# A hybrid attention and Hyena backbone on one core: order of work in the filters' network, the gates, the rows of maxima and the value weights

## The chip, the cores and the metric

The kernel runs on one core of one Trainium2 chip. The metric is the device time of one execution in microseconds (us): the median of the runs.

The core has five engines with queues of their own: TensorE (PE, with its weight loads, PEld), VectorE (DVE), ScalarE (ACT), GpSimd (POOL) and SyncE (SP), which here issues nearly all DMAs. Each engine takes its instructions in order and waits where something that the next one needs is not there. All data is float32. Nearly all large products are made in three parts: each operand is split into a rounded high part (a copy to the type float32r) and a low part (the rest, by a subtraction), and high x high, high x low and low x high are summed.

## The reference, cut to what matters

Two layers over 1024 latent tokens of width 1024, with 256 context tokens that only attention reads.

```python
for i in range(2):
    shift, scale, gate = split(silu(c) @ ada_w[i] + ada_b[i], 3)          # modulations
    h_lat = rms_norm(x_lat, norm_w[i]) * (1 + scale) + shift              # h_ctx the same way, layer 0
    if i == 0:   # attention: 8 heads of GQA (2 key heads, rotary) and 8 heads of MLA
        q_a, k_a, v_a, c_q, c_kv, k_pe, g = split(h @ w_in)               # norms, rotary
        o = softmax(q k^T * scale) v          # 1024 queries, 1280 keys, 16 heads
        y = (o * silu(g)) @ w_out
    else:        # Hyena, order 2
        p = h_lat @ w_in                      # three streams with a short convolution, one gate
        z = parts[0]
        for o in range(2):
            z = parts[o + 1] * long_conv(z, k_f[:, o], skip[o])           # by Fourier transforms
        y = (z * silu(gate)) @ w_out
    x_lat = x_lat + gate * y
return rms_norm(x_lat, final_norm_w)

# filters of the long convolutions: a small network over positions, with decays
hid = sin(freq * (emb @ w1 + b1)); hid = sin(freq * (hid @ w2 + b2))
h = (hid @ w3 + b3) * exp(-t * abs(deltas)); kern = kern / sum(abs(kern)); k_f = rfft(kern)
```

## The kernel before

The program runs in stages, and the order of the work on PE, ACT, DVE and POOL is the order in which the instructions are written (or, for the two middle stages, in which a planner of generators hands them out). Only SP's order is left to the compiler's scheduler.

**Filters' network and ada weights (0 to about 32 us).** The positions' network runs on two halves of 512 positions, q = 1 first. sin_arg makes the argument of a Sin in seven DVE instructions (L460 to L466), hidden(q) takes the second Sin on ACT (L504), rounds it (L505) and subtracts for the low part Hl (L506), today on POOL for q = 1 and on DVE for q = 0. taps(n) multiplies the hidden values with the last weights (PE, L479 and L100 to L102); it is run for 32 steps, (p, gq) with p the block of 128 channels. Steps 0 and 1 need half 1 alone. decay makes the exponentials on ACT (L530), decayed the kernel tile on DVE (L535), norms the absolute sums (ACT L544, POOL L546), first_stage and second_stage the two stages of the filters' Fourier transform (PE L557 and L572), regroup and spectra move data by SP's DMAs.

In between, the generator modulations loads sixteen pieces of ada_w, 512 KB each, and multiplies them with silu(c) (PE, L217). It is pulled by hand: pull(mods, m) takes m steps, of which each issues the load of piece j + 4 and the four product records of piece j. PM says how many steps are pulled at four places. The pieces lie in five tiles in turn (tags ckh, ckl, kpe and two of xt), so the load of piece 14 overwrites piece 11, and so on. A row copy (L221), a transposition (L225) and small DVE instructions (L235, L236) end the generator. row_stats loads the ten tiles of token rows (SP L373, the tag xt again) and takes their sum of squares (ACT L380) in steps n = 1 to 10 of the loop over 38 steps n that follows.

**Projection and gates (about 245 to 485 us).** After four chunks of the attention's input projection, gates() makes the gate in 16 steps of 24 products: for step n it loads a weight tile wr of 512 KB (SP, L800), rounds it (ACT, L803) and subtracts for the low part wl (L804), on POOL for n < 8, else on DVE. wr, wh and wl have two buffers each. Beside it run elementwise (norms and the rotary steps of the queries, four pairs of tiles: DVE L922, POOL L838, DVE L839 and L840), latents and stacks, each handed out by the planner S after its yields (a cost on PE, a delay).

**Attention (about 485 to 1008 us).** 32 groups gi of one head and one half of the queries (q = gi % 2), five steps s each: scores(0) and scores(1), two or three products each (L1277), the exponential PT (ACT, L1294), products with the values of earlier PT in bursts of 16 records (L1180), sums of PT on POOL and DVE (L1187 to L1193). Ahead of it the maxima of the next group's scores are taken (PE L989 and L993, DVE L990 and L994), joined by max_all (DVE, L1008) at the end of s = 3, and max_rows, at s = 4, turns them on PE (L1023) and writes them as a row under the next group's queries (DVE, L1028). mla_prep makes the queries, keys and values of MLA beside it; its value weights are rounded (ACT L1506) and the low part uvl is taken on POOL (L1508) ahead of 30 products with the latents.

**Output projection, Hyena (1008 us to the end).** Not touched.

## Time and profile before

| | us |
|---|---|
| median of 3 runs | 1821.87 |
| lowest, highest | 1821.21, 1828.35 |
| the profiled execution | 1821.09 |
| its span, first to last instruction | 1819.3 |
| mean granted TensorE clock | 0.987 of full speed |

The profile is of one execution. The rows below give times from the span's start. "busy" is an engine's time inside instructions; "[0.67 <-DVE m L1008]" behind a row says that the engine stood idle for 0.67 us ahead of it and what ended that. In the rows by stretch the numbers behind the stretch are its length, then each engine's busy time (with its instructions), the granted clock, the DMA engines' busy share and the GB/s that they moved.

### The profile page before, as it was taken

How to read it: one execution, taken by the hardware profiler on the slowest of the kernel's cores; microseconds unless marked ns; L12 is line 12 of the kernel's file. 1: busy time of each engine (PE TensorE's matmuls, PEld its weight loads, DVE VectorE, ACT ScalarE, POOL GpSimd, SP SyncE). 2: the span in 40 equal slices, each digit the busy share in tenths (PEclk: the TensorE clock that was granted, in tenths of full speed). 3: DMA queues.
4: the chain of work that ended last, by engine and by line, in shares of the span. 5: the costliest groups of instructions: out<-in, count | busy, mean ns of one | idle time of the engine just before them, and what ended most of it. 6: DMA issues, size and time to landing. Idle time of an engine off the chain costs nothing.

```text
span 1819.3 us, 25906 instructions
## 1 busy us (share of the span) xinstructions
PE 1725.1 (95%) x9616; PEld 1346.1 (74%) x9616; DVE 1029.7 (57%) x1495; ACT 774.3 (43%) x1326; POOL 865.6 (48%) x615
## 2 busy tenths in 40 slices
PE   7999999998999999899999999999999999899898
PEld 2667789986766666666666788888888788788686
DVE  5557757446666665466565323456657555645743
ACT  5878711243545544544444333243343333332431
POOL 2457712534379777577776453234333333244400
PEclk9999999999999999999999999999999999999999
DMA  7766688232120010100010227568787778787633
GB/s 256 246 211 216 210 257 276 64 82 74 43 56 24 11 47 21 39 32 22 22 34 21 81 88 184 161 178 221 215 228 223 223 217 219 209 239 212 196 98 110
DMA packets 245709, 253.28 MB, mean 139 GB/s; under 512 B 30591, under 2 KB 195367, under 8 KB 245167
## 3 DMA queue, kind: packets, MB, share of 16 engines
q1 hardware_dynamic: 243408, 249.53, 46.4%
q10 hardware_dynamic: 2176, 2.10, 0.4%
q8 instruction: 76, 1.25, 0.3%
q14 instruction: 49, 0.40, 0.1%
HBM read 169.65 MB, written 61.94 MB: 127 GB/s over the span
## 4 chain that ended last, share of the span: by engine, by line
PE 57%; DVE 7%; DMA 5%; POOL 3%; issue 2%; ACT 2%; SPq 1%; DVEq 0%; POOLq 0%; ACTq 0%
PE pw L1277 8%; PE pw L102 8%; PE pw L100 8%; PE pw L101 8%; PE pv L1180 7%; DMA K<-Kd 4%; PE pq L989 3%; PE pq L100 2%; PE pq L101 2%; PE pq L102 2%; PE pq L1871 2%; PE pq L1854 2%; DVE mx L990 2%; PE pq L1212 1%; POOL wl L1712 1%
## 5 line engine op out<-in xcount | busy, mean ns | idle before, releaser
L1294 ACT ACTIVATE PT<-pw 128x1024 f32<-128x1024 f32 x160 | 163.7, 1025 | 171.8 <-PE pw L1277 160.4
L990 DVE TENSOR_REDUCE mx<-pq 128x1 f32<-128x512 f32 x256 | 170.9, 683 | 112.9 <-PE pq L989 111.1
L100 PE MATMUL pw<-h1h,wh 128*128 128x512 f32 x512 | 209.4, 409 | 0.0
L102 PE MATMUL pw<-h1h,wl 128*128 128x512 f32 x512 | 202.7, 396 | 4.4 <-POOL wl L1712 4.4
L101 PE MATMUL pw<-h1l,wh 128*128 128x512 f32 x512 | 201.2, 393 | 0.0
L1847 POOL TENSOR_TENSOR K<-K,skp 128x512 f32<-128x512 f32 x64 | 86.3, 1350 | 217.8 <-DMA K<-Kd 196.1
L1189 POOL TENSOR_TENSOR acc<-acc,PT 128x1024 f32<-128x1024 f32 x62 | 147.5, 2379 | 22.3 <-ACT PT L1294 20.7
L102 PEld LDWEIGHTS pw<-h1h,wl 128*128 128x128 f32 x512 | 96.8, 189 | 26.8 <-POOL wl L1712 5.3
L101 PEld LDWEIGHTS pw<-h1l,wh 128*128 128x128 f32 x512 | 97.0, 189 | 17.8
L546 POOL TENSOR_TENSOR kacc<-kacc,kabs 128x512 f32<-128x512 f32 x56 | 72.4, 1294 | 79.1 <-ACT kabs L544 77.2
L100 PEld LDWEIGHTS pw<-h1h,wh 128*128 128x128 f32 x512 | 97.0, 189 | 17.5
L1712 POOL TENSOR_TENSOR wl<-wr,wh 128x1024 fp32r<-128x1024 f32 x32 | 79.5, 2483 | 54.9 <-ACT wh L1711 54.9
L1857 DVE SCALAR_TENSOR_TENSOR cB<-pq,K 64x512 f32<-64x512 f32 x64 | 44.4, 693 | 107.0 <-DMA K<-Kd 38.5
L1827 ACT COPY caT<-pq 128x512 f32<-128x512 f32 x64 | 37.6, 588 | 146.0 <-PE pq L102 104.0
L1187 POOL TENSOR_TENSOR acc<-PT,PT 128x1024 f32<-128x1024 f32 x31 | 73.9, 2385 | 53.7 <-ACT PT L1294 50.4
L572 PE MATMUL pq<-au,FBk 128*128 128x256 f32 x256 | 68.6, 391 | 11.6 <-DVE kc L583 10.1
L1888 DVE TENSOR_TENSOR cil<-spare,cih 128x512 fp32r<-128x512 f32 x64 | 54.4, 888 | 44.3 <-ACT cih L1887 44.3
L1873 ACT COPY cbT<-pq 128x512 f32<-128x512 f32 x64 | 37.5, 587 | 95.4 <-PE pq L1871 49.7
L1180 PE MATMUL pv<-PT,Va 128*64 128x256 f32 x640 | 77.9, 385 | 0.0
L1180 PE MATMUL pv<-PT,Vm 128*64 128x256 f32 x640 | 77.7, 385 | 0.0
L1854 PE MATMUL pq<-cau,FB 128*128 128x128 f32 x512 | 69.7, 280 | 8.1 <-DVE cA L1860 7.0
L1871 PEld LDWEIGHTS pq<-cA,GB 128*128 128x128 f32 x512 | 68.3, 195 | 11.8 <-issue 6.5
(449 smaller groups left out, 4705.8 us busy)
## 6 DMA issues: line engine op xcount, KB each, us to landing
K<-Kd SPq DMA_DIRECT2D x128, 256.0 KB
au<-aT SPq DMA_DIRECT2D x128, 128.0 KB
space<-in_ada_w_dram SPq DMA_DIRECT2D x32, 512.0 KB
wr<-in_hy_w_in_dram SPq DMA_DIRECT2D x32, 512.0 KB
ad<-caT SPq DMA_DIRECT2D x64, 256.0 KB
cau<-ad SPq DMA_DIRECT2D x32, 512.0 KB
bd<-cbT SPq DMA_DIRECT2D x32, 512.0 KB
spare<-bd SPq DMA_DIRECT2D x64, 256.0 KB
```

The lines of the kernel that those rows point to most:

```text
L100: nc.tensor.matmul(ps, lh, rh, start=start, stop=False)
L101: nc.tensor.matmul(ps, lh, rl, start=False, stop=False)
L102: nc.tensor.matmul(ps, ll, rh, start=False, stop=stop)
L990: nc.vector.reduce_max(m[:, i, j:j + 1], ps, axis=AX.X)
L1180: nc.tensor.matmul(ps[64 * e:64 * e + 64, 0:256], vals[:, 2 * s + j], PT[:, j, 256 * e:256 * e + 256], start=s == 0 and j == 0, stop=s == ...
L1189: eng.tensor_tensor(accs[gi], accs[gi], PT, ALU.add)
L1277: nc.tensor.matmul(ps[:, 512 * j:512 * j + 512], l[:, kt * P:(kt + 1) * P], r, start=i == 0, stop=i == len(passes) - 1)
L1294: nc.scalar.activation(PT, ps.rearrange("p (a q) -> p a q", q=512), AF.Exp, scale=SC_A if kind == 0 else SC_M)
L1712: nc.gpsimd.tensor_tensor(wl, f(r), f(wh), ALU.subtract)
L1847: nc.gpsimd.tensor_tensor(K[:, 0], K[:, 0], B["skp"].unsqueeze(1).to_broadcast([P, 4, P]), ALU.add)
L1854: nc.tensor.matmul(ps[:, i * P:(i + 1) * P], FB[:, 4 * uc + i, :], au[:, 4 * (uc % 2) + i, :], start=True, stop=True)
L1871: nc.tensor.matmul(ps[:, i * P:(i + 1) * P], GB[:, 4 * uc + i, :], A1[:, i, :], start=True, stop=True)
```

## The change

It changes the order of work at four places, and the engine of two subtractions. No product and no byte is added or removed.

- The ada steps are pulled later: PM goes from 3, 3, 5, 3 to 2, 1, 3, 3, and the loop's first three turns pull two instead of one. Nine instead of fourteen of the sixteen are ahead of the loop. hidden(1) is moved between the two arguments; the low part of half 1 goes to DVE, that of half 0 to POOL; the split of the first coefficients moves ahead of half 1's argument.
- In gates() the load of step n + 2 is issued at step n, apart from the rounding and subtraction of step n + 1; the low parts 2, 4 and 6 stay on POOL, 1, 3, 5 and 7 go to DVE.
- max_rows stays between scores(0) and scores(1) for even groups and goes behind scores(1) for odd ones. Its planner's cost of 0.1 falls away.
- The low part uvl of the value weights goes from POOL to DVE.

```diff
-PM = 3, 3, 5, 3
+PM = 2, 1, 3, 3
...
-            (nc.vector, nc.gpsimd)[q].tensor_tensor(Hl[:, c], Hr[:, c], f(Hh[:, c]), ALU.subtract)
-
-        args[1] = sin_arg(pss[1], b2)
+            (nc.gpsimd, nc.vector)[q].tensor_tensor(Hl[:, c], Hr[:, c], f(Hh[:, c]), ALU.subtract)
+
         nc.scalar.copy(ind, indr)
         split_coefs(0)
+        args[1] = sin_arg(pss[1], b2)
+        hidden(1)
         args[0] = sin_arg(pss[0], b2)
-        hidden(1)
         hidden(0)
...
-            pull(mods)
+            pull(mods, 2 if n < 3 else 1)
...
-            wt = {}
+            wt, raw = {}, {}
 
             def load(n):
                 if n < 16:
                     i = n % 8
-                    r = wp.tile([P, NK, P], F32, tag="wr", bufs=2, name=nm("wr"))
-                    nc.sync.dma_start(r, win[:, :, 1184 + i * P:1184 + (i + 1) * P])
+                    raw[n] = wp.tile([P, NK, P], F32, tag="wr", bufs=2, name=nm("wr"))
+                    nc.sync.dma_start(raw[n], win[:, :, 1184 + i * P:1184 + (i + 1) * P])
+
+            def split(n):
+                if n < 16:
+                    r = raw.pop(n)
                     wh = wp.tile([P, NK, P], F32R, tag="wh", bufs=2, name=nm("wh"))
                     wl = wp.tile([P, NK, P], F32R, tag="wl", bufs=2, name=nm("wl"))
                     nc.scalar.copy(wh, r)
-                    (nc.gpsimd if n < 8 else nc.vector).tensor_tensor(wl, r, f(wh), ALU.subtract)
+                    (nc.gpsimd if n in (2, 4, 6) else nc.vector).tensor_tensor(wl, r, f(wh), ALU.subtract)
                     wt[n] = wh, wl
 
+            load(1)
             wt[0] = box["g0"][1:]
             for n in range(16):
                 hf, i = divmod(n, 8)
-                load(n + 1)
+                split(n + 1)
+                load(n + 2)
...
-                if s == 4 and gi + 1 < 32:
+                if s == 4 and gi % 2 == 0:
                     max_rows(gi + 1)
-                    cost += 0.1
                 scores(1, todo)
+                if s == 4 and gi % 2 and gi + 1 < 32:
+                    max_rows(gi + 1)
...
-        nc.gpsimd.tensor_tensor(uvl, r, f(uvh), ALU.subtract)
+        nc.vector.tensor_tensor(uvl, r, f(uvh), ALU.subtract)
```

## Rows read from the trace of the kernel before

**Rows 1.** The page: each engine's busy time, share of the span and instructions, and the shares of the lines in the chain of work that ended last.

```profile
PE 1725.1 (95%) x9616; PEld 1346.1 (74%) x9616; DVE 1029.7 (57%) x1495; ACT 774.3 (43%) x1326; POOL 865.6 (48%) x615
...
PE pw L1277 8%; PE pw L102 8%; PE pw L100 8%; PE pw L101 8%; PE pv L1180 7%; DMA K<-Kd 4%; PE pq L989 3%; PE pq L100 2%; PE pq L101 2%; PE pq L102 2%; PE pq L1871 2%; PE pq L1854 2%; DVE mx L990 2%; PE pq L1212 1%; POOL wl L1712 1%
```

**Rows 2.** Busy time by stretch: two of the first 60 us.

```profile
10.00:15.00 5.00, 2.19 (x10) 0.42 (x8) 3.61 (x7) 1.82 (x5) 0.00 (x0) 1.00 1.00 402
...
30.00:60.00 30.00, 27.12 (x144) 17.92 (x145) 14.56 (x19) 28.16 (x71) 15.04 (x13) 1.00 0.74 244
```

**Rows 3.** The timeline of the first 40 us: PE, ACT, DVE, POOL and SP's queue (start, duration, engine, line, operation).

```profile
14.84 0.40 ACT L342 CAST b<-b3r 2x256 fp32r<-2x256 f32 x1
...
16.70 0.81 DVE L460 TENSOR_SCALAR sa<-pq,vecs 128x512 f32<-128x512 f32 x1 [2.92 <-PE pq L497]
...
20.44 1.27 ACT L504 ACTIVATE Hr<-sa 64x512 f32<-64x512 f32 x2 [5.20 <-DVE sa L466]
...
22.93 2.57 POOL L506 TENSOR_TENSOR Hl<-Hr,Hh 128x1024 fp32r<-128x1024 f32 x1 [7.19 <-ACT Hh L505]
...
25.45 0.39 PE L479 MATMUL pw<-b,ind 128*128 128x256 f32 x1
...
26.54 1.27 ACT L504 ACTIVATE Hr<-sa 64x512 f32<-64x512 f32 x2 [3.76 <-DVE sa L466]
...
29.00 0.42 SPq L499 DMA_DIRECT2D FKc<-in_FK_dram  x1
...
31.52 1.23 DVE L535 TENSOR_TENSOR kern<-pw,dec 128x1024 f32<-128x1024 f32 x1 [1.29 <-ACT dec L530]
...
32.51 1.05 PE L217 MATMUL pada<-adaw,sT 128*32 128x512 f32 x4 [1.56 <-DMA adaw<-in_ada_w_dram]
...
33.83 1.27 ACT L530 ACTIVATE dec<-dlt,tng 128x128 f32<-128x128 f32 x4
...
35.48 1.88 PE L557 MATMUL pq<-kern,FKc 128*128 128x512 f32 x4
...
36.53 0.59 ACT L559 COPY aT<-pq 128x512 f32<-128x512 f32 x1 [1.43 <-PE pq L557]
...
39.53 1.06 ACT L380 ACTIVATE xs<-xs 128x1024 f32<-128x1024 f32 x1
```

**Rows 4.** The gates: SP's loads of the weights (their number at the end), the timeline of PE and DVE, and a stretch with the granted clock.

```profile
371.84 87.47 SPq L800 DMA_DIRECT2D wr<-in_w_in_dram  x15
...
413.51 0.80 PE L102 MATMUL pw<-h,wl 128*128 128x512 f32 x1 [3.69 <-POOL wl L804]
...
415.00:420.00 5.00, 5.00 (x15) 3.97 (x14) 2.28 (x3) 0.00 (x0) 4.18 (x5) 0.59 0.32 94
...
419.61 3.40 DVE L840 TENSOR_TENSOR pD<-rt,rt 128x1024 f32<-128x1024 f32 x1 [2.68 <-POOL rt L838]
...
428.13 1.23 DVE L840 TENSOR_TENSOR pD<-rt,rt 128x1024 f32<-128x1024 f32 x1 [2.72 <-POOL rt L838]
...
429.27 1.22 DVE L804 TENSOR_TENSOR wl<-wr,wh 128x1024 fp32r<-128x1024 f32 x1
...
430.55 0.49 PE L102 MATMUL pw<-h,wl 128*128 128x512 f32 x1 [2.70 <-DVE wl L804]
```

**Rows 5.** Attention: PE's waits for the joined maxima, in the first and in the second kind of head (us in total, times, longest); the timeline of PE at two transpositions; the durations of the row's writing (ns, least, median, most; first and last start).

```profile
PE pq L1023 <- DVE m L1008: 4.0, 6, 0.8
...
PE pq L1023 <- DVE m L1008: 2.7, 7, 0.4
...
537.39 0.40 PE L1277 MATMUL pw<-Qa,K 128*128 128x512 f32 x1
...
537.62 0.39 PE L1277 MATMUL pw<-Q,K 128*128 128x512 f32 x1
...
538.69 0.27 PE L1023 MATMUL pq<-ident,m 128*4 128x128 f32 x1 [0.67 <-DVE m L1008]
...
539.36 1.95 PE L1180 MATMUL pv<-PT,Va 128*64 128x256 f32 x16
...
840.45 0.27 PE L1023 MATMUL pq<-ident,m 128*4 128x128 f32 x1 [0.38 <-DVE m L1008]
...
L1028 DVE TENSOR_TENSOR QA<-pq,dneg x16: 682/684/684, 723.6 to 988.7; 4x512 fp32r<-4x512 f32 x16
```

**Rows 6.** The timeline around the value weights' low part, ACT, POOL, DVE and PE, and the stretch behind it with its granted clock.

```profile
740.04 0.60 ACT L1506 CAST uvh<-uvr 128x512 fp32r<-128x512 f32 x1
...
740.28 2.35 POOL L1189 TENSOR_TENSOR acc<-acc,PT 128x1024 f32<-128x1024 f32 x1 [2.54 <-ACT PT L1294]
...
741.23 0.17 DVE L1008 TENSOR_REDUCE m<-mx 128x4 f32<-128x12 f32 x1
...
744.05 1.26 POOL L1508 TENSOR_TENSOR uvl<-uvr,uvh 128x512 fp32r<-128x512 f32 x1
...
745.37 0.79 PE L101 MATMUL pq<-uvl,ckh 128*128 128x512 f32 x1 [4.15 <-POOL uvl L1508]
...
745.00:750.00 5.00, 4.63 (x11) 3.67 (x12) 0.00 (x0) 1.76 (x3) 3.85 (x3) 0.50 0.27 105
```

**Rows 7.** SP's queue: the load that stands in turn 22 of the loop, and the page's line on the loads of the filters' spectra.

```profile
45.81 0.38 SPq L613 DMA_DIRECT2D w<-in_w_in_dram  x1
...
K<-Kd SPq DMA_DIRECT2D x128, 256.0 KB
```

## The prediction

> **What bounds the kernel now.** I read the page first, then the chain of waits, then busy time by stage, then the timeline of the four places that the diff touches. TensorE is busy 95% of the span, and its products hold the largest shares of the chain that ended last [rows 1]. No other engine is near it, so an edit pays only where PE stood still, or ran at half clock, for something that the edit moves. The reader should look for PE's stalls beside each edit. In the first 40 us PE is not the bound: a chain over VectorE, ScalarE and the loads sets the pace, and from 30 to 60 us ScalarE is busy 28.16 of 30 us [rows 2]. In the gates PE waits for a low part twice (3.69 and 2.70 us), the first time followed by half clock [rows 4]. In attention it waits for the maxima of odd groups [rows 5]. Once it waits 4.15 us for the low part of the value weights, and then runs at 1.2 instead of 2.4 GHz [rows 6].
>
> **Head (modulations behind the filters' network).** Today half 1's Sin starts at 20.44, its low part 2.49 us later on GpSimd, taking 2.57, and the first taps at 25.45 [rows 3]. Afterwards VectorE first makes the coefficients' low part (ScalarE's cast ends at 15.24; I take 15.65 for its end), then half 1's argument (16.70 to 20.44, 3.74 us), to 19.4; the low part starts at 21.9 and ends at 23.1 (1.22 on VectorE, as in [rows 4]). The taps come 2.3 us earlier. But half 0's argument now stands behind that low part on VectorE: 23.1 + 3.74 = 26.85 against 26.54 today. So the first kernel tile comes 0.3 us later and ends at 33.1 instead of 32.75. No gain has reached ScalarE yet.
>
> Next, the product that waited 1.56 us for ada weights at 32.51 no longer stands ahead of the first-stage products: they start at 33.1 instead of 35.48. ScalarE's copies of them come after the next decays (33.83 + 1.27 = 35.1 today, 35.4 then) instead of at 36.53: ScalarE is 1.1 us ahead, and its first sum of squares could start at 38.4 instead of 39.53. But that needs the first token rows, and their load stands in SP's queue behind ada loads. With five tiles, load 14 waits for the product of piece 11, which moves from ahead of the decays to behind the first-stage products: 33.1 + 1.88 + some 0.9 of its 1.05 = 35.9. Today load 14 left just ahead of the one at 29.00, at 28.5, and its product ran at 32.51: 4.0 us. So it lands at 39.9. The token rows behind it are another 0.5 MB, 1.3 us at the 402 GB/s of the best stretch [rows 2]: 41.15. ScalarE stands for 2.7 us and is then **1.6 us later** than today. From there it has hardly a gap to 60 us, so the shift stays. I take +1.6 because written order is what SP's row shows in the head: the table FKc, which needs nothing, left at 29.00 behind the blocked loads. Bounds: -1.1 (row loads pulled ahead) and +2.9 (load 15, 0.5 MB, also in front). The five product steps that move into the loop's first turns, 1.05 us or less each on PE, lie under ScalarE's full stretch: nothing; without that cover 2 us. The generator's end on VectorE moves two turns back, where I see no wait for it: nothing.
>
> The Trainium skill (DMA: Bandwidth & Descriptors, Anatomy of one DMA) gives a load 2.0 us plus its bytes at 436 GB/s, on GpSimd's path; an estimate from it is 3.2 us for 512 KB, where the row has 4.0. By it the head would cost 0.8 instead of 1.6 us.
>
> **Gates.** Loading two steps ahead changes nothing that I can price: SP already spreads the fifteen loads over 87 us, each leaving when its buffer is free [rows 4], and the first, the only one that ScalarE waits for, keeps its place: 0. What counts is that low parts 1, 3, 5 and 7 go from GpSimd to VectorE (1.22 each). PE waits for the chain of rotary steps (VectorE product, four GpSimd products, VectorE sum, the next pair), with the low parts between. A VectorE sum next to a GpSimd low part takes 3.40 us, without one 1.23 [rows 4]. After pairs 0 and 2 this saves 2.17 and adds 1.22: 2 x -0.95. Pair 1 keeps low part 6 on GpSimd. Low parts 1 and 3 stand in front of VectorE's sums of squares and push the start by an estimated 0.25 each: +0.5. Low part 8, at 429.27 today, comes at 427.9: **-1.4 us**, and PE's restart at 430.55 with it. The long stall (3.69) is cut into shorter ones, and the half clock at 415 to 420 should go; neither is added, since the wait for low part 8 lies behind them and would take it back. Queued behind the low parts on VectorE is the next rotary product, which is in the sum. Bounds: 0 (the clock falls again) and -1.9 (no push at the start).
>
> **Rows of maxima.** For odd groups the transposition of the maxima now stands behind both score products instead of between them. Today PE goes 1.07 us from a score product to the transposition, of which the product itself is 0.23: 0.84 lost, 0.67 of it a wait. In the second kind of head the wait is 0.38, so 0.54 lost [rows 5]. There are 6 and 7 such waits; the other transpositions have none and stay or lose nothing. Moved, the second half's products fill the wait: two, 0.47 of 0.84, in the first kind; three, 0.70, all of 0.54, in the second. 6 x 0.47 + 7 x 0.54 = **-6.6 us**. It could hold up the next group's second score product, which needs the row that VectorE writes (0.68 us) after the transposition; between lie 1.95 us of value products: nothing, and 0.3 us a group if the burst weren't there. The planner's charge of 0.1 per group falls away; its other streams restart at group ends, so 0, +-1.
>
> **Low part of the value weights on VectorE.** Its rounded part is ready at 740.64, but GpSimd comes to it at 744.05, behind a sum (740.28, 2.35 us) and a scaling. VectorE is free from 741.40. It would read two tiles of SBUF beside GpSimd's sum, and as in the gates wait for that sum's end, 742.63, then take half of 1.22 for half the columns: 743.25. PE restarts at 743.35 instead of 745.37: -2.0. Its wait shrinks from 4.15 to 2.1 us; after 2.70 the clock stayed up (430.55), after 3.69 it fell [rows 4]. So the half clock should go too: eleven products at 0.42 us [rows 6] instead of 0.23, and the wait's restart, -2.35. Together **-4.35**; bounds -2.0 (clock falls) and -5.5 (no block).
>
> The Trainium skill (Advanced Engine Details and Errata, Mode Summary) says that GpSimd and VectorE's two-port modes block each other. A subtraction of two float32 tensors is in none of these modes; by the letter it would start at once, for 1.2 us more. The rows (3.40 against 1.23) speak for the block.
>
> **Sum.** +1.6 - 1.4 - 6.6 - 4.35 = -10.75. Against the profiled execution's 1821.09 us (span 1819.3) that is 1810.3. The median of the runs lies 0.8 above the profiled one: **1811.1**.
>
> **Rivals.**
> B: SP's order is planned anew, and the token rows' loads go ahead of the blocked ada loads. For it: SP doesn't always follow the text (the load that stands in turn 22 left at 45.81, six us after turn 1's sum of squares) [rows 3, 7]. Head -1.1 instead of +1.6: 1808.4.
> C: waits come back. The clock falls after the shorter stalls too (value weights -2.0, gates 0), and half of the maxima's gain returns as a wait for a buffer or a row: +1.6 - 0 - 3.3 - 2.0 = -3.7, 1818.2. For it: the new stalls in the gates stand closer together. Against it: no other engine in attention is near full [rows 1].
> D: slower than before. With new times in the planner SP's order changes in the second half too, where loads of the filters' spectra hold 4% of the chain [rows 1, 7]. If each of the 64 pairs leaves one place later, each costs one issue, 0.4 us: +25.6, 1836.7. It decides from 27 pairs on; slower by over 0.5% takes 50. Against it: nothing of that half is edited.
>
> **How the numbers follow.** A, the forecast, 0.46 (own range 1808 to 1814); B 0.25; C 0.24; D 0.05. B with the far bounds of the value weights and the gates gives 1805; C gives 1818; about 2 in 10 lie outside. 0.5% (9.1 us) is about what a measurement of this kernel can tell from no change, so faster means under 1812.8: three quarters of A, B, a little of C: 0.62. Slower by over 0.5%: 0.04. Within: 0.34.
>
> **What would show it.** Head: taps at 23, first sum of squares at about 41 after a wait for the token rows (B: 38.4, no wait). Gates: VectorE's sums after pairs 0 and 2 at 1.23 us; PE's restart at step 8 some 1.4 us earlier, counted from the gates' start; clock at its full level throughout. Maxima: no wait at transpositions of the second kind, about 0.3 us in the first. Value weights: low part 2 to 3 us after the cast, then full clock. I am wrong if attention doesn't shrink by about 11 us, or if the head moves by more than 3.

## The result and the profile after

| | before | after |
|---|---|---|
| median of five runs each (us) | 1827.38 | 1811.57 |
| lowest, highest | 1821.21, 1830.2 | 1808.1, 1814.33 |
| profiled execution, its span | 1821.09, 1819.3 | 1808.1, 1806.3 |

The ratio after to before is 0.9933, 95% interval 0.9912 to 0.9955: faster by 0.45 to 0.88%. The median of 1811.57 stands 0.5 us from the 1811.1 predicted. The two medians of the table are 15.8 us apart; with later runs the median of before settles at 1821.5 (of 33 runs, 1813.5 to 1831.0), so the gain is some 10 us. Executions of one kernel spread over 6 us and more; so below, stages are compared over several profiled executions. The profiled execution of x7_value_cover (2101 us at a granted clock of 0.75) and one execution of x11_cover_keys_early (8427 us) are far slower than the rest and are left out, as are two such of before (2223 and 2809 us).

The page of after [for before: rows 1], busy time and chain by engine. PE is busy 95% as before; DVE's busy time is 8.6 us longer, POOL's 14.5 shorter.

```profile
PE 1723.1 (95%) x9616; PEld 1346.7 (75%) x9616; DVE 1038.3 (57%) x1500; ACT 774.5 (43%) x1326; POOL 851.1 (47%) x610
...
PE 64%; DMA 10%; DVE 10%; issue 6%; POOL 5%; ACT 3%; SPq 1%; POOLq 0%; DVEq 0%; ACTq 0%
```

**Head** [rows 2, 3]. The timeline of after, DVE's low part of half 1, PE's first taps, and the first products:

```profile
22.23 1.23 DVE L506 TENSOR_TENSOR Hl<-Hr,Hh 128x1024 fp32r<-128x1024 f32 x1 [2.54 <-ACT Hh L505]
...
23.51 0.58 PE L102 MATMUL pw<-w3h,Hl 128*128 128x256 f32 x1 [0.54 <-DVE Hl L506]
...
26.59 3.72 PE L217 MATMUL pada<-adaw,sT 128*32 128x512 f32 x20
...
33.30 1.98 PE L557 MATMUL pq<-kern,FKc 128*128 128x512 f32 x4 [0.91 <-DVE kern L535]
```

ACT's sums of squares and SP's loads in the same execution, and two stretches (columns as in rows 2; the last three are granted clock, DMA share and GB/s):

```profile
39.94 1.06 ACT L380 ACTIVATE xs<-xs 128x1024 f32<-128x1024 f32 x1 [1.74 <-DMA xs<-in_ctx_dram]
...
50.39 1.06 ACT L380 ACTIVATE xs<-xs 128x1024 f32<-128x1024 f32 x1 [1.49 <-DMA xs<-in_x_dram]
```
```profile
31.08 1.40 SPq L373 DMA_DIRECT2D xs<-in_ctx_dram  x2
36.31 0.82 SPq L199 DMA_DIRECT2D adaw<-in_ada_w_dram  x2
```
```profile
25.00:30.00 5.00, 5.00 (x28) 2.19 (x27) 1.91 (x4) 2.89 (x4) 0.47 (x1) 0.65 0.12 20
35.00:40.00 5.00, 5.00 (x29) 2.71 (x28) 1.74 (x2) 3.26 (x10) 3.48 (x4) 1.00 0.90 352
```

Three things are to be seen. The taps come at 23.5 and the first-stage products at 33.3, as worked out. From 25 to 30 us the DMA engines move 20 GB/s: five ada steps stand behind the taps on PE (26.59), and until they run no tile comes free for a load. And SP did not keep the written order: the first token rows left at 31.08, ahead of the last ada loads (36.31), but were 8.9 us on the way to the sum of squares that waited for them.

**Gates** [rows 4]. DVE's rotary sums and low parts, PE's last wait, and the stretch behind the longest wait:

```profile
401.85 1.23 DVE L846 TENSOR_TENSOR pD<-rt,rt 128x1024 f32<-128x1024 f32 x1 [2.72 <-POOL rt L844]
...
410.71 3.36 DVE L846 TENSOR_TENSOR pD<-rt,rt 128x1024 f32<-128x1024 f32 x1 [2.72 <-POOL rt L844]
419.17 1.23 DVE L846 TENSOR_TENSOR pD<-rt,rt 128x1024 f32<-128x1024 f32 x1 [2.71 <-POOL rt L844]
...
427.78 1.22 DVE L808 TENSOR_TENSOR wl<-wr,wh 128x1024 fp32r<-128x1024 f32 x1
```
```profile
429.05 0.50 PE L102 MATMUL pw<-h,wl 128*128 128x512 f32 x1 [1.60 <-DVE wl L808]
```
```profile
415.00:420.00 5.00, 5.00 (x17) 3.94 (x17) 2.26 (x3) 0.00 (x0) 3.79 (x4) 0.73 0.21 64
```

The sums of pairs 0 and 2 take 1.23 us; pair 1, with low part 6 still on POOL, is held as before. The clock fell again (0.73 here), behind PE's wait of 2.07 us for low part 6.

**Maxima** [rows 5]. PE's waits for the joined maxima from 484 to 727 us (from 752 to 992 there is none in the list), and a transposition of the first kind:

```profile
PE pq L1029 <- DVE m L1014: 1.0, 4, 0.3
```
```profile
536.08 0.40 PE L1283 MATMUL pw<-Q,K 128*128 128x512 f32 x1
536.37 0.17 DVE L1014 TENSOR_REDUCE m<-mx 128x4 f32<-128x12 f32 x1
536.68 0.27 PE L1029 MATMUL pq<-ident,m 128*4 128x128 f32 x1 [0.21 <-DVE m L1014]
536.88 1.95 PE L1186 MATMUL pv<-PT,Va 128*64 128x256 f32 x16
```

**Value weights** [rows 6].

```profile
735.93 2.35 POOL L1195 TENSOR_TENSOR acc<-acc,PT 128x1024 f32<-128x1024 f32 x1 [2.55 <-ACT PT L1301]
...
736.96 1.88 DVE L1515 TENSOR_TENSOR uvl<-uvr,uvh 128x512 fp32r<-128x512 f32 x1
...
738.89 0.79 PE L101 MATMUL pq<-uvl,ckh 128*128 128x512 f32 x1 [2.02 <-DVE uvl L1515]
```

The subtraction ends 0.56 us behind POOL's sum, and the wait is 2.02 instead of 4.15 us. The stretch behind it still has some products at 1.2 GHz, though fewer than in before:

```profile
740.00:745.00 5.00, 5.00 (x20) 4.05 (x19) 0.00 (x0) 3.47 (x6) 3.47 (x2) 0.81 0.28 98
```

**Where the span's 13.0 us went** in this pair of profiles, by the starts of the same ACT instructions: gates reached (first rounded latents) 379.97 and 380.10, +0.1; from there to attention's first exponential 106.45 and 104.79, -1.7; from there to group 16's first exponential 245.94 and 243.11, -2.8; to group 18's first, which holds the value weights and one transposition, 46.98 and 43.47, -3.5; to the output stage's first sum of squares 239.96 and 236.76, -3.2; to the end 800.00 and 798.09, -1.9. The prediction's four places hold -11.1 of it.

### The profile page after: what moved, and what is told of

It is laid out like the page before. It is cut to its first block, busy times and chain, and to the rows that moved or that the text cites. A ratio compares the mean times of both kernels' runs of the same rounds, so it can differ in the third digit from the quotient of the medians.

```text
span 1806.3 us, 25904 instructions
## 1 busy us (share of the span) xinstructions
PE 1723.1 (95%) x9616; PEld 1346.7 (75%) x9616; DVE 1038.3 (57%) x1500; ACT 774.5 (43%) x1326; POOL 851.1 (47%) x610
## 4 chain that ended last, share of the span: by engine, by line
PE 64%; DMA 10%; DVE 10%; issue 6%; POOL 5%; ACT 3%; SPq 1%; POOLq 0%; DVEq 0%; ACTq 0%
PE pw L102 9%; PE pw L1283 9%; PE pw L101 9%; PE pw L100 9%; PE pv L1186 7%; DMA K<-Kd 4%; PE pq L995 3%; PE pq L100 3%; PE pq L101 3%; PE pq L102 2%; DMA Kd<-kc 2%; PE pq L1861 2%; PE pq L1878 2%; PE pq L572 1%; DVE mx L996 1%
## 5 line engine op out<-in xcount | busy, mean ns | idle before, releaser
L1195 POOL TENSOR_TENSOR acc<-acc,PT 128x1024 f32<-128x1024 f32 x62 | 147.3, 2376 | 22.4 <-ACT PT L1301 20.8
```

The lines of the kernel that those rows point to most:

```text
L1195: eng.tensor_tensor(accs[gi], accs[gi], PT, ALU.add)
```

## The experiments

All stages below are measured between the same ACT instructions.

| kernel | fifth sum of squares | gates reached | gates | groups 0 to 15 | groups 16, 17 | groups 18 to 31 | second half |
|---|---|---|---|---|---|---|---|
| before | 57.03 | 379.97 | 106.45 | 245.94 | 46.98 | 239.96 | 800.00 |
| x2_maxima_alone | 56.16 | 379.69 | 108.01 | 243.17 | 44.39 | 236.75 | 802.87 |
| x3_low_parts_alone | 57.82 | 380.65 | 104.85 | 245.95 | 46.20 | 239.88 | 800.79 |
| x4_value_low_part_alone | 61.37 | 379.73 | 108.02 | 245.89 | 41.45 | 239.89 | 796.16 |
| x1_head_undone | 60.77 | 379.56 | 104.82 | 243.21 | 40.93 | 236.76 | 800.82 |
| x6_steps_back | 60.69 | 380.39 | 104.89 | 243.12 | 41.85 | 236.78 | 800.68 |
| x9_together | 60.04 | 381.30 | 103.85 | 243.22 | 44.36 | 236.78 | 807.16 |
| after | 59.42 | 380.10 | 104.79 | 243.11 | 43.47 | 236.76 | 798.09 |
| x0_changed_again | 60.63 | 383.61 | 104.84 | 243.19 | 41.22 | 236.77 | 800.74 |
| x8_low6 | 59.30 | 384.35 | 103.91 | 243.12 | 41.56 | 236.75 | 800.00 |
| x7b_cover_again | 60.02 | 385.27 | 104.83 | 243.21 | 44.30 | 236.78 | 800.03 |
| x11_cover_keys_early | 59.86 | 381.77 | 104.80 | 243.20 | 42.59 | 236.78 | 802.95 |
| x10_all_behind | 59.70 | 378.88 | 104.80 | 246.30 | 41.47 | 236.76 | 799.79 |

The first five rows have the old head, the next two the old steps with the new order of the network, the last six the changed head. Kernels with the same code there repeat within 0.1 us in the gates (but for those of before, 106.45 or 108.0) and in attention (but for groups 16 and 17); the head, the way to the gates and the second half do not.

In the head the seven executions with the ada steps as before (x6 and x9 among them) part from the six with the steps pulled later, by starts in the traces (us):

| | steps as before | steps later |
|---|---|---|
| first-stage products start | 34.5 to 39.8 | 33.2 to 33.4 |
| first sum of squares | 38.6 to 43.8 | 39.0 to 40.5 |
| from the second sum to the third | 4.2 to 5.2 | 6.2 to 7.6 |
| from the seventh to the tenth | 20.0 to 20.4 | 20.8 to 21.6 |
| from the tenth to the gates reached | 288.5 to 293.6 | 288.5 to 294.4 |

**x2_maxima_alone**

```diff
-                if s == 4 and gi + 1 < 32:
+                if s == 4 and gi % 2 == 0:
                     max_rows(gi + 1)
-                    cost += 0.1
                 scores(1, todo)
+                if s == 4 and gi % 2 and gi + 1 < 32:
+                    max_rows(gi + 1)
```

> The kernel before with the rows of maxima alone changed (transposition of odd groups behind both score products, the planner's 0.1 gone). Theory (each wait is filled by the products behind it, 0.47 us in the first kind of head, 0.54 in the second): attention shortens in steps at odd groups, 6.4 us in all, no other stage moves; total about 1815 where the kernel before has 1821. The wait for the value weights' low part stays at 4.15 us and its half clock at about 6.8. Rival C of the prediction (half comes back as waits for a buffer or a row): 3.3 us, total about 1818. Rival (the planner places other work anew without the 0.1): the order on PE changes outside the rows of maxima and the steps are not of one size.

Measured: median 1816.35 against 1821.5 (ratio 0.9967, 0.995 to 0.9984). Groups 0 to 15 are 2.77 us shorter than before, groups 18 to 31 3.21, and PE's waits for the joined maxima are the four of 0.3 us or less that after has. Nothing comes back: rival C falls for this part. The planner did not move other work: in attention PE's instructions start in the same order as in before, but for the fifteen transpositions of odd groups. The wait for the value weights was 2.86 here, not 4.15, with nothing changed there. What varies is the load of these weights. ACT waits for it ahead of the scaling, the cast and the exponential that POOL's sum needs. The first row is of before, the second of x2:

```profile
738.50 0.73 ACT L1502 ACTIVATE uvr<-uvr,kw 128x512 f32<-128x512 f32 x1 [3.85 <-DMA uvr<-in_w_ukv_dram]
...
734.90 0.72 ACT L1503 ACTIVATE uvr<-uvr,kw 128x512 f32<-128x512 f32 x1 [1.75 <-DMA uvr<-in_w_ukv_dram]
```

Counted from group 16's first exponential, the cast starts at 7.67 us in before and at 6.34 here. Over all executions it lies between 6.3 and 7.7, after's profile (7.69) being the latest.

**x3_low_parts_alone**

```diff
-                    (nc.gpsimd if n < 8 else nc.vector).tensor_tensor(wl, r, f(wh), ALU.subtract)
+                    (nc.gpsimd if n in (2, 4, 6) else nc.vector).tensor_tensor(wl, r, f(wh), ALU.subtract)
```

> The kernel before with the engines of low parts 1, 3, 5, 7 of the gates alone changed (DVE instead of POOL); loads as before. Theory (the chain of rotary steps waits less, the order of loads is worth nothing): the whole gain of the gates comes from here: low part 8 at 427.8 instead of 429.3, attention starts 1.5 to 1.65 us earlier than before, the half clock at 413 to 420 shrinks from about 6.8 to 3.4 us; total about 1820 where the kernel before has 1821.5. Rival (the loads two steps ahead brought it): less than 0.3 us here.

Measured: median 1818.38 (ratio 0.998, 0.9959 to 1.0001), which alone is not told apart from before. The gates take 104.85 us, as in after (104.79): the engines bring the whole gain, the loads two steps ahead nothing. The gates of before took 106.45 in its own profile and 108.0 in x2 and x4: there the clock fell after the second wait too. The stretch from 430 to 435 us in before, then in x2:

```profile
430.00:435.00 5.00, 4.45 (x21) 3.68 (x22) 4.08 (x5) 1.16 (x2) 2.05 (x3) 1.00 0.42 109
...
430.00:435.00 5.00, 4.75 (x16) 3.90 (x17) 3.60 (x4) 0.46 (x1) 2.35 (x4) 0.67 0.50 115
```

**x4_value_low_part_alone**

```diff
-        nc.gpsimd.tensor_tensor(uvl, r, f(uvh), ALU.subtract)
+        nc.vector.tensor_tensor(uvl, r, f(uvh), ALU.subtract)
```

> The kernel before with the value weights' low part alone changed (DVE instead of POOL). Theory (the wait shrinks by 2.1 us, but two microseconds are still enough for the clock to fall, for a shorter time): PE restarts 2.5 us after its first product with the rounded part instead of 4.6, the products run at 1.2 GHz for about 3 us instead of 5 to 7, the stage gains 3.0 us; total about 1818.5 where the kernel before has 1821.5. Rival (the prediction's step: the half clock goes with the shorter wait): 4.35 us gained. Rival (here the subtraction starts at another time relative to GpSimd's sum and is held up by it, 3 us or more): 1 us or less.

Measured: median 1819.72 (ratio 0.9988, 0.997 to 1.0007), which alone is not told apart from before. The timeline of POOL, DVE and PE, and the two stretches behind:

```profile
740.25 2.38 POOL L1189 TENSOR_TENSOR acc<-acc,PT 128x1024 f32<-128x1024 f32 x1 [1.23 <-ACT PT L1294]
...
742.52 0.17 DVE L1008 TENSOR_REDUCE m<-mx 128x4 f32<-128x12 f32 x1
742.60 0.69 DVE L1508 TENSOR_TENSOR uvl<-uvr,uvh 128x512 fp32r<-128x512 f32 x1
743.34 0.50 PE L101 MATMUL pq<-uvl,ckh 128*128 128x512 f32 x1 [0.84 <-DVE uvl L1508]
```
```profile
740.00:745.00 5.00, 4.09 (x31) 2.82 (x31) 3.01 (x6) 2.67 (x6) 4.67 (x3) 1.00 0.07 28
745.00:750.00 5.00, 5.00 (x24) 4.12 (x23) 0.00 (x0) 4.34 (x8) 2.94 (x2) 1.00 0.19 77
```

PE goes on at 743.34, where the prediction has 743.35, but that is a coincidence. DVE joins the maxima until then (742.52), and by the time it comes to the subtraction POOL's sum is ending (742.63): nothing holds it, and it takes 0.69 us. PE waits 0.84 us, not 2.1. Group 16 began 1.3 us later than in before, and its load came earlier in the group (ACT waited 2.02 us for it instead of 3.85), so that POOL's sum ran at the same time as in before. Counted from group 16's first exponential, PE goes on at 9.70 us here and in x1, and at 11.70 in x2 and x3, whose load came as early; with the late load it is 10.89 (after) against 13.00 (before). So DVE is worth 2.0 to 2.1 us either way. The clock stays up. Groups 16 and 17 gain 5.5 us on before's profile, of which some 1.3 are the load's. The first theory (half clock after two microseconds) is not put to the test, since no wait was that long.

That the subtraction is held by POOL's sum is seen where it starts beside it, as in after and in x0 (POOL, then DVE):

```profile
738.68 2.36 POOL L1195 TENSOR_TENSOR acc<-acc,PT 128x1024 f32<-128x1024 f32 x1 [1.66 <-ACT PT L1301]
740.59 1.00 DVE L1515 TENSOR_TENSOR uvl<-uvr,uvh 128x512 fp32r<-128x512 f32 x1
```

In seven executions (after, x0, x6, x7b, x8, x10, x11) it starts 0.45 to 1.32 us ahead of the sum's end and takes 1.00 to 1.88 us; each time it ends 0.54 to 0.56 us behind the sum.

**x1_head_undone**

```diff
-PM = 2, 1, 3, 3
+PM = 3, 3, 5, 3
...
-            pull(mods, 2 if n < 3 else 1)
+            pull(mods)
```

and the order and engines of hidden and sin_arg as before.

> The changed kernel with the head as it was before (steps pulled 3, 3, 5, 3, one per turn, order and engines of the filters' network as before); gates, rows of maxima and value weights stay changed. Theory (the head loses: the later ada steps leave the DMA engines empty from 25 to 30 us, 20 GB/s in the changed kernel against 216 before, so token rows come late and ScalarE runs 2.4 us late at 60 us): first square sum at 39.5 instead of 39.9, the one in the seventh place at 53.2 instead of 55.6, end of the filters' stage 1.25 us earlier than in the changed kernel. The half clock ahead of the gates, which lasted about 6.8 us before and 3.4 in the changed kernel, goes with the times of the head and comes back: the gates start within 0.2 us of the changed kernel, and the total stays within 1 us of it (about 1811.6). Rival 1 (the short half clock has nothing to do with the head): the 1.25 us are kept, gates start 1.2 us earlier, total about 1810.3. Rival 2 (the head's change pays somewhere behind the head): gates or attention later by 2 us or more, total 1813.5 or more.

Measured: median 1812.79 of 11 runs from 1800.7 to 1819.6 (ratio 0.9943, 0.9919 to 0.9968). The first sum of squares came at 42.31, not at 39.5, with the very head of before: my theory had read a difference of 2.4 us between two executions as the work of an edit. The gates were reached at 379.56; the long half clock ahead of them did not come back. It is no mark of the old head: it stands in the traces of before, x7b and x11 alone, of which two have the changed head.

**x0_changed_again**: the changed kernel, unedited.

> The changed kernel once more, unedited, to see how far one execution stands from the next. Theory (the head's times are set by when loads land, and differ between executions of the same code by up to 5 us, as five executions with the old head showed: first square sums at 38.6 to 43.8; the projection swallows this, all five reach the gates' first rounded latents at 379.6 to 380.7): the first square sum falls anywhere between 38 and 44, the first rounded latents at 380 +-0.6, from there to attention's first exponential 104.8 +-0.1 (three executions of the changed gates), the wait for the value weights' low part 2.0, with or without half clock behind it. Median within 2 us of 1811.6. Rival (the changed head itself costs 2.4 us at 60 us): the square sums come at the same 39.9 and 54.6 again.

Measured: median 1811.51 (ratio 0.9942, 0.9924 to 0.9961). First sum of squares at 39.75, gates reached at 383.61: the second half of the theory on the head falls, since the projection does not swallow what the head is late, and the first half does not hold for this head, whose first sum came at 39.0 to 40.5 in six executions. The rival has the first sum right (39.9); the sum that it puts at 54.6 came at 55.82. Gates (104.84) and attention repeat; the wait for the value weights was 1.16, with full clock.

**x6_steps_back**

```diff
-PM = 2, 1, 3, 3
+PM = 3, 3, 5, 3
...
-            pull(mods, 2 if n < 3 else 1)
+            pull(mods)
```

> The changed kernel with the ada steps alone pulled as before (3, 3, 5, 3, one per turn); the new order and engines of the filters' network stay. Theory (the steps pulled late empty the DMA engines from 25 to 30 us, and the head as a whole is swallowed by the projection): over 150 GB/s from 25 to 30 us where the changed kernel has 20; the first rounded latents at 380 +-0.6 all the same; median within 2 us of the changed kernel's. Rival 1 (late steps are worth what the medians of the first three parts leave over, 1.2 us): median 1.2 us above the changed kernel. Rival 2 (they cost 2.4 us): median 2.4 below it, gates reached at 377.7.

Measured: median 1810.9 (ratio 0.9941, 0.9924 to 0.9957); no difference in the median against x0, on the same chip. The stretch from 25 to 30 us moves 224 GB/s: the hole was made by the late steps.

```profile
25.00:30.00 5.00, 3.87 (x28) 2.09 (x24) 1.89 (x4) 2.91 (x4) 0.49 (x1) 1.00 0.69 224
```

Yet the fifth sum of squares comes at 60.69, no earlier than in after. The time is lost at another place: with the old steps PE's first-stage products stand behind ada products that wait for their loads, and ACT behind those.

```profile
32.94 1.92 PE L217 MATMUL pada<-adaw,sT 128*32 128x512 f32 x4 [1.78 <-DMA adaw<-in_ada_w_dram]
...
38.38 2.02 PE L557 MATMUL pq<-kern,FKc 128*128 128x512 f32 x4
...
39.58 0.59 ACT L559 COPY aT<-pq 128x512 f32<-128x512 f32 x1 [4.00 <-PE pq L557]
```

Of the seven executions with the old steps, the clock fell with that wait in five, and their first-stage products start at 36.3 to 39.8; in the other two (before, x2) it stayed up, and they start at 35.5 and 34.5. That is the spread of the old head. The gates were reached at 380.39.

**x8_low6**

```diff
-                    (nc.gpsimd if n in (2, 4, 6) else nc.vector).tensor_tensor(wl, r, f(wh), ALU.subtract)
+                    (nc.gpsimd if n in (2, 4) else nc.vector).tensor_tensor(wl, r, f(wh), ALU.subtract)
```

> The changed kernel with low part 6 of the gates on DVE too (2 and 4 stay on POOL). Theory (a DVE sum beside a POOL low part is held to its end, 3.36 against 1.23 us, so the chain of rotary steps saves 2.13 and pays 1.22): the sum at 410.7 takes 1.23 us, low part 8 comes 0.9 us earlier counted from the first rounded latents, attention starts 0.9 us earlier (103.9 from there instead of 104.8), 1.7 earlier if the half clock behind the wait of 2.07 goes as well. Rival (PE then waits for low part 6 as much as it gained, since DVE comes to it only behind the sum): low part 6 ends 0.5 us or less earlier than at 412.98, but nothing changes at low part 8: 0. Median 0 to 1.7 below the changed kernel's.

Measured: median 1810.22 (ratio 0.9927, 0.9905 to 0.9949). The sum of pair 1 takes 1.23 us, and the gates 103.91 instead of 104.83: -0.92, as priced. PE's wait for low part 6 is 2.19, longer than the 2.07 before, and the gain is there all the same, since the chain of rotary steps ends in low part 8. The clock stays at its full level through the gates here and in x9, where each of the eight other executions with the new engines has one fall; the expected 1.7 for that did not come. So a half clock ahead of the wait for low part 8 costs nothing, as the prediction had it.

```profile
414.99 1.23 DVE L846 TENSOR_TENSOR pD<-rt,rt 128x1024 f32<-128x1024 f32 x1 [2.75 <-POOL rt L844]
416.13 1.22 DVE L808 TENSOR_TENSOR wl<-wr,wh 128x1024 fp32r<-128x1024 f32 x1
```
```profile
417.40 0.49 PE L102 MATMUL pw<-h,wl 128*128 128x512 f32 x1 [2.19 <-DVE wl L808]
```

**x7_value_cover and x7b_cover_again** (the same kernel)

```diff
-                burst = s in (1, 4) if gi == 16 else (gi + s) % 2
+                burst = s == 1 if gi == 16 else (gi + s) % 2
```

> The changed kernel with one more edit: group 16 takes its burst of value products at step 1 alone, not at 1 and 4, so that its step 4 (six score products and the transposition, some 1.6 us of PE) no longer waits for the value weights and goes between their low part and their products. Theory (PE's wait there is a gap that other work can fill; the half clock comes and goes with the wait): PE's wait for the low part falls from 2.0 to 0.5 us or less, no product behind it runs at 1.2 GHz, attention is 1.5 us shorter than in an execution of the changed kernel without half clock there and 2.4 shorter than in the profiled one; median 1.5 to 2.4 below the changed kernel's. Rival (the burst put off comes back: the exponential of the next step waits for one of the five PT buffers): PE waits for ACT by 1 us or more in the first step of group 17, gain 0.5 us or less.

> The kernel of the run before (group 16 bursts at step 1 alone, so that its step 4 covers the value weights' low part) once more, for a profile at full clock: its median came 4 us above the changed kernel's, where 1.5 to 2.4 below was expected. Theory (the cover was spent twice: group 17 may not start before the keys of the next head are there, and their weights are loaded only behind the value products; that load and its split were hidden under the step that now goes ahead): PE waits 3 us or more for the rounded key weights behind the last value product, where the changed kernel waits 0.53, and the half clock follows that wait; the low part itself is waited for 0.5 us or less. Rival (the exponential of group 17 waits for a PT buffer): the longest wait of PE or ACT from the value products to group 17 is for value products, not for the key weights. Rival 2 (the 4 us were chance): median within 1.5 of the changed kernel's 1811.5.

Measured: medians 1815.4 and 1813.27 (ratios 0.996, 0.9943 to 0.9977, and 0.995, 0.9933 to 0.9967): nothing gained, if anything lost. The low part is no longer waited for. In its place, behind the last value product of x7b, and the stretch that follows:

```profile
754.24 0.45 PE L100 MATMUL pq<-ckh,ukh 128*64 128x512 f32 x1 [3.74 <-ACT ukh L1349]
```
```profile
755.00:760.00 5.00, 5.00 (x20) 3.77 (x20) 2.83 (x5) 2.97 (x6) 3.23 (x2) 0.66 0.03 7
```

Group 16's step had been the cover of the next head's key weights; moved ahead of the value products it covers the low part, and the key weights stand bare: 3.74 us and half clock, 44.30 us for the two groups where full-clock executions of the changed code take 40.9 to 41.9.

**x11_cover_keys_early**: the same burst, and the key weights of head 1 loaded and split earlier (key_stack is parted into key_load, key_split and the rest, which the cut leaves out):

```diff
+        rk = key_load(1)
         yield 0, UV
         nc.scalar.activation(r, r, AF.Identity, scale=kw)
...
             nc.scalar.copy(Vm[:, kt, :], ps)
+            if kt == 2:
+                parts = key_split(rk)
...
-        yield from key_stack(1)
+        yield from key_stack(1, parts)
```

> The kernel with the covered low part, and the next head's key weights loaded right behind the value weights' load and split behind the third value product, instead of both behind the tenth. Theory (the key weights are the wait that took the gain): no wait for the key weights, 0.5 us or less for the low part, full clock from the value products to group 18; from the first exponential of group 16's step 0 to that of group 18's step 0, attention is 1.5 to 2.5 us shorter than in an execution of the changed kernel without half clock there; median 1809 to 1810. Rival (the PT buffers or the planner's other work took it): median still 1814 or more.

Measured: median 1816.1 (ratio 0.9967, 0.9954 to 0.9981). The wait for the key weights is gone, and the next thing in the row is late, the keys themselves:

```profile
751.41 0.55 PE L995 MATMUL pq<-K,QA 128*128 128x512 f32 x1 [1.78 <-DVE kc L1378]
```

The two groups take 42.59 us, again with half clock. So the key weights were the first wait behind the cover, not the only one: the theory held for its cause and fell for its gain.

**x10_all_behind**

```diff
-                if s == 4 and gi % 2 == 0:
-                    max_rows(gi + 1)
                 scores(1, todo)
-                if s == 4 and gi % 2 and gi + 1 < 32:
+                if s == 4 and gi + 1 < 32:
                     max_rows(gi + 1)
```

> The changed kernel with the rows of maxima behind both score products in even groups too. Theory (even groups had no wait at the transposition, so there is nothing to fill; in odd groups the products fill the wait): attention as long as in the changed kernel within 0.5 us, no wait at any transposition but the remains of the first kind; median within 1.5 of 1811.5. Rival (even groups gain as well, or parity is needless): 3 us less. Rival 2 (the place between the products is better where the maxima are ready: the row comes later and the next group's second product waits for it): 0.2 us or more a group, 3 us more. Its head is that of the changed kernel: a further execution of it.

Measured: median 1820.04 of 12 runs from 1809.8 to 1829.0 (ratio 0.9989, 0.9971 to 1.0008). In the profile, groups 0 to 15 take 246.30 instead of 243.2 us, groups 18 to 31 236.76 as in after. PE's list of waits from 484 to 727 us has a new line:

```profile
PE pw L1283 <- DVE Q L1034: 2.4, 8, 0.3
```

Rival 2 holds, in the first kind of head alone: 8 even groups, each 0.3 us of wait for the row, 3.1 us in all with the restarts. Behind an even group's fifth step there is no burst of value products to hide the row; behind an odd group's there is. In the second kind no group loses. The median is some 8 us above the changed kernel's, though the profile is of the fastest of the twelve; 3 of these are explained, the rest is not.

**x9_together**: steps as in x6, low part 6 as in x8, burst and keys as in x11.

> What the runs point to, in one kernel: the changed kernel with the ada steps pulled as before (new order of the network kept), low part 6 of the gates on DVE, the value weights' low part covered by group 16's step 4, and the next head's key weights loaded early. Theory (the parts lie in different stages and add up): gates reached at 380 +-0.6, from there 103.9 to attention, attention 2 us shorter than the changed kernel's; 1 to 2.5 us of the ada steps, 0.9 of the gates and 2 of the cover below the changed kernel's median: 1806 to 1808. Rival (the ada steps are worth nothing, and the second half's own spread hides the rest): 1809 to 1811.

Measured: median 1809.67 of 6 runs from 1802.5 to 1818.5 (ratio 0.9938, 0.9915 to 0.9961). Gates 103.85, as in x8; groups 16 and 17 44.36 with the same 1.78 us wait as in x11; second half 807.16, the longest of all with code that no edit touches. It is not told apart from the changed kernel; what can be kept of it is low part 6.

## Why the prediction was right, point by point

**The whole.** -10.75 was forecast; the stages of the profiled pair up to 1008 us gave -11.1, and the medians some -10. The terms were not all sized so well: by means over the executions of each code the head cost 2.4 (forecast 1.6), the gates gave 2.7 (1.4), the maxima 6.5 (6.6) and the value weights 3.9 (4.35). That these again make -10.7 is luck in part: the misses on the head and the value weights cancel the one on the gates.

**Head, +1.6.** The steps up to PE's taps and first-stage products hold (23.5 and 33.3). Three steps failed. First, the token rows' load does not stand behind ada loads in SP's queue, with the first sum of squares at 41.15: the loads left ahead (31.08), as rival B had them, and the sums came at 39.0 to 40.5 in six executions. But rival B's gain did not come either: the rows waited 1.74 us more. Second, "from there it has hardly a gap" is wrong: ACT waits again for token rows at the third sum, 1.49 us in after (50.39) and 1.5 to 2.9 in all six executions with the late steps, against 0.9 at most with the old ones. Third, today's 39.53 is one execution's: the old head gives anything from 38.6 to 43.8.

The fifth sum of squares came at 59.3 to 60.6 (mean 59.8, six executions) against 56.2 to 61.4 with the old head (mean 58.6, five): +1.2. From the seventh to the tenth sum the late steps lose 1.0 us more, without an overlap. By the gates it is 382.3 (378.9 to 385.3) against 379.9 (379.6 to 380.7): +2.4, with a standard error of 1.0. The profiles x1 to x4 were taken on another chip than x0 and x6 to x11, so this difference may be the chip's in part. The medians of x0 and x6 (1811.5, 1810.9, on one chip) do not show it. That the late steps empty the DMA engines is shown by x6, and that the third sum's rows come late with them by the table; through which queue is not shown, nor what the time from the seventh to the tenth sum goes to.

The Trainium skill (DMA: Bandwidth & Descriptors, Anatomy of one DMA) gives 3.2 us for the rows, as an estimate from its figures for GpSimd's path. Here, on SP's queue, 8.9 us lay between the issue and the end of the wait. In that time the DMA engines moved 304 GB/s, some 2.7 MB or five times the tile: that the loads in front made the price is likely, but not shown.

**Gates, -1.4.** Low part 8 came at 427.78 where 427.9 was forecast. The profiled pair gave -1.7. Mean over executions: 107.5 before (before, x2, x4), 104.83 with the new engines (eight, within 0.1), -2.7, beyond the bound of -1.9. The step that failed: "after 2.70 the clock stayed up". It did in one execution and fell in two of the same code (x2, x4). That the half clock at 415 to 420 goes was wrong as well: 0.73 there in after, and one fall in the gates of each of the eight. That it would be taken back by the wait for low part 8 was right (x8). Loads two steps ahead at 0: right (x3).

**Maxima, -6.6.** Right in size and place: 2.8 in the first kind, 3.2 from group 18 on, and -6.5 in all if the seventh transposition of the second kind, in group 17, gained the same 0.5; x4 and x1, whose value weights come alike and which differ there in the maxima alone, are 0.52 apart in groups 16 and 17. The remaining waits of 0.3 us in the first kind were forecast, and so was the price of the row where no burst stands behind it (0.3 us a group, x10).

**Value weights, -4.35.** The restart's -2.0 is right: 2.1 with the late load (before, after), 2.0 with the early one (x2 and x3, x4 and x1). So is its reason, the block, for the late load, as after's 1.88 us and the six executions like it show. Where the load is early, it is DVE's own queue that sets the start, and x4's 743.34 is luck. What the forecast left out is that the load sets the wait: 4.15 in before's profile, 2.86 and 2.85 in x2 and x3. Of the half clock's 2.35, the eleven products give 2.1; the rest, put down to the wait's restart, stands in no row. It went in x4, x1, x0, x6, x8 and x10 and stayed in after's profile, where it cost some 1.4 us (43.47 against 41.85 in x6, whose load was 0.26 us less late). Means of groups 16 and 17, with 0.54 taken off where the transposition is the old one: 45.5 before (three executions), 41.6 changed (seven): -3.9.

The Trainium skill's Mode Summary (Advanced Engine Details and Errata) ties the block to two-port modes; after's row speaks against the letter of it, with 1.88 us for an instruction that takes 0.69 in x4. The same page's section GPSIMD Details adds "or with two SBUF inputs", and with that the rows agree.

**Rivals.** B named SP's order rightly and its gain wrongly. C's half clock came in after's own profile, at a lower price (value weights -3.0, gates -1.7), but not its return of waits in attention. D did not happen: the second half took 796 to 807 us over thirteen executions of the same code, before at 800.0; the -1.9 of the profiled pair lies well inside that spread.

## What to carry to other kernels

A wait is worth what can be put under it: the transposition gained because products with nothing to wait for stood next to it, and in even groups of the first kind the same move lost, because nothing stood behind to hide its result. Cover can be spent only once: before moving a step under a stall, ask what it covers now. A forecast that lands on a row's time is not yet a mechanism: in x4 the restart was met to 0.01 us with another wait in force. And before a difference of two profiles is given a cause, profile the same code again: here stages repeated to 0.1 us in attention and missed by 5 us in the head.

## What the runs showed of the hardware

The fall of the clock does not follow from the length of PE's wait alone. In the gates with the new engines PE waits 2.07 to 2.10 us for low part 6 in eight executions; the clock fell behind that wait in four of them and stayed up in the other four, where it fell behind the next one (2.67 to 2.69 us). PE's row and the stretches behind it, of x0, where it stayed, then of x1, where it fell:

```profile
416.58 0.50 PE L102 MATMUL pw<-h,wl 128*128 128x512 f32 x1 [2.08 <-POOL wl L808]
415.00:420.00 5.00, 3.42 (x15) 2.80 (x16) 4.97 (x3) 0.60 (x1) 2.64 (x2) 1.00 0.41 104
420.00:425.00 5.00, 2.44 (x11) 1.64 (x9) 2.29 (x4) 1.53 (x2) 2.69 (x4) 1.00 0.00 0
...
412.51 0.49 PE L102 MATMUL pw<-h,wl 128*128 128x512 f32 x1 [2.08 <-POOL wl L808]
415.00:420.00 5.00, 4.91 (x17) 3.58 (x15) 2.30 (x3) 0.52 (x2) 3.60 (x4) 0.77 0.15 45
```

It also stayed up behind a wait of 2.19 (x8, low part 6), and behind 2.70 in the gates of before it stayed once and fell twice, with the same instructions. A forecast should carry such a half clock as a chance, here some 1.5 us each where no other wait stands behind it (gates of before 108.0 or 106.45; value weights 43.47 or 41.85), and nothing where one does (x8). The Trainium skill (TensorE: Matmul & The Clock Gate, What's actually happening) says that the count of slow products at a kernel's start varies between runs of one kernel; these runs show the like at waits in the middle.

DVE's subtraction of two SBUF tensors beside a POOL sum is held until the sum is over, however much of the sum is left: it took 1.88 us in after and 1.00 in x0, with its end 0.54 to 0.56 us behind POOL's in seven executions. In x4, x1 and x9 it came only as the sum ended, and took 0.69.
